# A decoder step on one core: the second norm from per-block sums, rows scaled by a diagonal product, a written order in front of the MLP, and sample values as one run per step

## The chip, the cores and the metric

One core of one Trainium2 chip runs the whole step in one launch. The metric is the device time of one execution in microseconds (us), lower is better. Engines are named as the profile names them: PE (matrix engine; PEld is its weight load), DVE (vector), ACT (scalar), POOL (GpSimd) and SP (the queue that issues most loads).

## The reference, cut to what matters

One layer, 256 prompt tokens and 8 sample tokens (one new token each, with states), D = 2048, FF = 8192, all in float32.

```python
h = rmsnorm(x, g_pre_mix) * (1 + sc1) + sh1
z = h @ w_in                       # three mixers: gMLP gating, HGRN2, GLA
merged = sum(sigmoid(z_gate[n]) * (branch[n] @ w_branch[n]) for n in range(3))
out = merged @ w_out
x = x + gt1 * rmsnorm(out, g_post_mix)
h2 = rmsnorm(x, g_pre_mlp) * (1 + sc2) + sh2
y2 = square(relu(h2 @ w_mlp_up)) @ w_mlp_down
x = x + gt2 * rmsnorm(y2, g_post_mlp)
```

`sh1, sc1, gt1, sh2, sc2, gt2` are six slices of `silu(c) @ w_ada + b_ada`, one row for the prompt and one for each sample. The outputs are the new rows, the final HGRN2 and GLA states of the prompt, the updated states of the samples (`f*S + k v^T`), and the normalised gating rows.

## The kernel before, in words

**Products.** Activations lie with channels on the partitions: 16 channel tiles of 128, each with 264 columns (256 prompt tokens, 8 samples). Every weight block is split into a rounded part `whi` (ACT copy, L112) and a remainder `wlo` (DVE subtract, L109), the activations likewise, and each 128x128 weight tile takes three products (L543 to L545). `granule` (L533) works off one 512 KB block of weights: 24 products. `linear` (L601) makes 256 output columns from 16 channel tiles in four granules, 96 products, and calls `background` after each. `Stream` (L482) keeps blocks loaded up to 5 granules ahead and split up to 2 ahead; there are buffers for 6 half blocks of split weights, and at the end of each granule `ahead` emits the split of the block three further on, into the buffers that this granule gives free.

**Side work.** `background` (L588) advances a granule counter `now` and pumps three queues of generators, in this order: the mixers (`bg`), the samples' states (`bs`) and the remaining rounds of `w_ada` (`ba`), each at a rate in `RATES`. `slot` (L556) puts waiting small products of the mixers and the samples on PE, and one step of an `ada_round` (L275: four products of 128x512 against the condition, eight records in the trace).

**Samples.** `samples_r` (L943) takes one step per sample and 512 state columns. A step fetches the state two steps ahead, asks for the values one step ahead (`values`, L961: a DMA on POOL's queue that hands one sample's value rows, kept in DRAM as `vs_d`, to all 128 partitions), waits until `now` is `FETCHED` = 3 granules past both issues, scales (ACT L983), adds (DVE L985), writes the state back, and queues the products with `q` for a slot. There are four state buffers, so a fetch waits on POOL until the products of an earlier sample (L576) have run. `finish` (L1179) is called in front of a branch: it drains the queues, closes the samples' output with a norm (L995 to L997) and transposes it on PE (L1186). `bs` and `ba` are drained there without granules in between.

**Around the change.** After the third branch comes `w_out`: eight blocks of `linear`, each followed by `gated_rows` (L1293): squares of the block (ACT), the block times the gate (ACT and DVE), four transposes to token rows (L711) and their copies to `og` (L1304, L1312). The last block's squares stay apart and go into the norm's sums as separate products (L1319, L1321: nine of them). `norms` then computes `r1 = rsqrt(mean)` by a bit trick and three Newton rounds on DVE (`rstd_small`, L178: eleven small instructions). The rows are `x1 = x + og*r1` (L1349), the second norm squares `x1` on ACT (L212), sums the samples' squares on DVE and PE, and runs `rstd_small` again; the rows times `r2` (L1358, L1359) are transposed (32 transposes, L228), and `modulate` (L354) makes `h2`, its rounded part and its remainder. Into that stretch `fill` puts steps of the sixth `ada_round`; its first 12 of 32 weight tiles were loaded during `w_out` (`N_PRE`), the others go through two buffers `araw`. What is left of the round goes to `ba` and runs beside the MLP at 0.2 steps per granule. Then `up(0)`, `up(1)`, `down(0)`, and so on.

**Order.** From the start of the mixers to the end of the last branch PE and POOL run in written order (`manual_schedule`), and the compiler's scheduler orders the other engines. From L1283 on it orders all engines by its own estimate. At the end `norms` runs a third time, and eight pieces of 128x512 (L1416, all DVE) make the output rows, which SP and ACT write.

Of the kernel before, what the change touches and what calls it, by code (L numbers as in the profile page):

```python
# [15 lines left out]
P = 128  # L16
# [20 lines left out]
RATES = ((1.7, 0.4, 0.27), (1.5, 0.4, 0.27), (1.2, 0.4, 0.27), (1.0, 0.4, 0.27))  # L37
# [11 lines left out]
FILL = (4.0, 4.0)  # L49
# [11 lines left out]
def hybrid_step_kernel(  # L61
# [141 lines left out]


    def norm_rows(x, xs, xsn, r):
# [148 lines left out]
    def modulate(dst, src, xs, k0, n, A, B, hi, lo):  # L354

        for j in range(n):
            k = k0 + j
            if j % 2 == 0:
                V.tensor_scalar(dst[:, j, 0:NP], src[:, j, :], A[:, k, 0:1], B[:, k, 0:1], ALU.mult, ALU.add)
            else:  # L360
                S.activation(dst[:, j, 0:NP], src[:, j, :], AF.Identity, scale=A[:, k, 0:1], bias=B[:, k, 0:1])
# [87 lines left out]
    def plan():  # L449

        out, k0 = [], 0
        for n in CHUNKS:
            for gi in range(0, len(begin), 4 // n):
                out.append((win, k0, n, begin[gi][0], 4 // n * CW))
            k0 += n
        for c0 in (6144, 6400, 6656, 6912):
            out += blocks(win, 0, KT, c0)
        out += blocks(win, 0, KT, 9216, P)
        for s in range(4):
            out += blocks(win, 0, KT, 7168 + s * CW)  # L460
        for n in range(N_BRANCH):
            if n:
                g0 = 5120 if n == 1 else 8192
                for s in range(4):
                    out += blocks(win, 0, KT, g0 + s * CW)
            for m in range(8):
                out += blocks(win, 0, KT, 9232 + n * D + m * CW) + blocks(w_branch[0, n], 0, 8, m * CW)
        for m in range(8):
            out += blocks(w_out[0], 0, KT, m * CW)
        for f in range(NFB + 1):  # L470
            if f < NFB:
                for m in range(FB // CW):
# [393 lines left out]
    vs_d = dp.tile([3, 8, NS, P], F32, tag="vs_d", name="vs_d")  # L866
# [76 lines left out]
    def samples_r(G):  # L943
# [4 lines left out]
        fs = tmp([P, 4, NS], f"fs{G.i}", 1)  # L948
# [24 lines left out]
        for n, (b, h0) in enumerate(steps):  # L973
# [6 lines left out]
            yield lambda: now[0] >= max(ahead[0][1], vals[0][1]) + FETCHED  # L980
# [20 lines left out]
    def mixer_r(G):  # L1001
# [12 lines left out]
        nc.gpsimd.dma_start(vs_d[G.i, 0:4 * nj].rearrange("k b v -> (k b) v"), vs)  # L1014
# [276 lines left out]
    parts = []  # L1291

    def gated_rows(m, src, Gv, rows):  # L1293
# [4 lines left out]
        g = tmp([P, 2, NP], "gt")  # L1298
        S.activation(g[:, 0, :], src[:, 0, 0:NP], AF.Copy, scale=Gv[:, k, 0:1])
        V.tensor_scalar(g[:, 1, :], src[:, 1, 0:NP], Gv[:, k + 1, 0:1], None, ALU.mult)  # L1300
        pt = to_tokens(g)
        mul(gs[:, k:k + 2, :], src[:, :, NP:NT], Gv[:, k:k + 2, 1:NC])
        c0 = (m % 4) * CW
        S.copy(rows[0][m // 4][:, c0:c0 + CW].rearrange("p (m f) -> p m f", m=2), pt[:, 0])  # L1304
        if m == 0:
            add(sqacc, sq[:, 0, :], sq[:, 1, :])
        elif m < 7:
            add(sqacc, sqacc, sq[:, 0, :])
            add(sqacc, sqacc, sq[:, 1, :])
        else:  # L1310
            parts[:] = [sqacc, sq[:, 0, :], sq[:, 1, :]]
        V.tensor_copy(rows[1][m // 4][:, c0:c0 + CW].rearrange("p (m f) -> p m f", m=2), pt[:, 1])  # L1312

    def norms():

        ps = sm([P, 2 + NS])
        for t in range(2):
            for i, v in enumerate(parts):
                T.matmul(ps[:, t:t + 1], v[:, t * P:(t + 1) * P], ones[:, 0:1], start=i == 0, stop=i == 2)  # L1319
        for i, v in enumerate(parts):  # L1320
            T.matmul(ps[:, 2:2 + NS], ones, v[:, NP:NT], start=i == 0, stop=i == 2)  # L1321
        r = tmp([P, 2 + NS], "nr", 1)
        rstd_small(ps, 1.0 / D, r)
        return r[:, 0:2], r[:, 2:2 + NS]

    og = [[blk([P, 1024]) for _ in range(2)] for _ in range(2)]
    mH, mL = tiles(mh), tiles(ml)
    pre = []
    for m in range(8):
# [6 lines left out]
        gated_rows(m, linear(w_out[0], 0, KT, m * CW, CW, mH, mL), G1, og)  # L1336
# [4 lines left out]
    fill = Queue()  # L1341
    fill.g.append(ada_round(5, pre))
    r1, r1s = norms()
    fill.pump(FILL[0])
    mul(gs, gs, r1s.unsqueeze(1).to_broadcast([P, KT, NS]))
    add(xsT, xsT, gs)
# [9 lines left out]
    for hf in range(2):
        for c in (slice(0, 512), slice(512, 1024)):
            S.activation(xn[0][hf][:, c], x1[0][hf][:, c], AF.Copy, scale=rx[:, 0:1])  # L1358
            V.tensor_scalar(xn[1][hf][:, c], x1[1][hf][:, c], rx[:, 1:2], None, ALU.mult)  # L1359
        for k in range(8 * hf, 8 * hf + 8, 2):  # L1360
            ps = transposed(xn, k)
            q, js = k // 4, slice(k % 4, k % 4 + 2)
            modulate(tmp([P, 2, NT], "vt"), ps, xsn, k, 2, A2, B2, h2h[q][:, js, :], h2l[q][:, js, :])
    ba.g.insert(0, fill.g[0]) if fill.g else None
# [24 lines left out]
    def down(f, ah, al):  # L1389
        for m in range(8):  # L1390
# [20 lines left out]
    r3, r3s = norms()  # L1411
    for t in range(2):
        for hf in range(2):
            for c0 in (0, 512):
                y = yt[t][hf][:, c0:c0 + 512]
                V.scalar_tensor_tensor(y, y, r3[:, t:t + 1], x1[t][hf][:, c0:c0 + 512], ALU.mult, ALU.add)  # L1416
# [58 lines left out]
```

## Time and profile before

| | |
|---|---|
| median of 3 runs | 1991.88 us (1988.23 to 1992.91) |
| profiled execution | 1991.31 us, of which its span is 1989.5 us |
| mean granted PE clock | 0.986 |
| DVE busy | 1190.4 us (60%) |
| ACT busy | 995.5 us (50%) |
| POOL busy, nearly all of it issuing DMAs | 86.0 us (4%) |
| `w_out` stage | about 1090 to 1183 us |
| last branch starts | about 929 us |
| read from HBM, written | 427.60 MB, 11.70 MB |

Times in the profile count from the start of the span. Matrix products are pipelined: a record of L543 lasts 0.28 us, but the next one starts 0.12 us later, so "busy" PE says little and the pace has to be read from start times or from the number of records in a stretch. `xN` is a number of instructions; in brackets or behind a bar stands how long the engine sat idle before a group and what ended most of that idle time. In the windows view `PEclk` is the clock granted to PE as a share of full speed. L-numbers are lines of the kernel before.

### The profile page before, as it was taken

To read this page: it belongs to the slowest core of one execution; us is meant where nothing else is said; L and a number is where in the kernel's file an instruction comes from. 1 tells how busy PE (TensorE), PEld (TensorE's weight loads), DVE (VectorE), ACT (ScalarE), POOL (GpSimd) and SP (SyncE) were. 2 spreads that over 40 slices of the span, in tenths; PEclk is the share of its full clock that TensorE was granted. 3 is DMA by queue.
4 is the path that set the end of the run, shared out by engine and by line. 5 is a ranking of instruction groups with operands and counts; after the bars stand their busy time and mean duration, and the time that the engine had idled before them with its cause. 6 is when DMAs were issued, how large, how long until landed. Compare 5 with 4: busy or idle time off the path is not lost.

```text
span 1989.5 us, 42035 instructions
## 1 busy us (share of the span) xinstructions
PE 1927.4 (97%) x16972; PEld 1819.9 (91%) x16972; DVE 1190.4 (60%) x2092; ACT 995.5 (50%) x1773; POOL 86.0 (4%) x128
## 2 busy tenths in 40 slices
PE   6999999999999999998999999999999999999997
PEld 4889999889989988997999987999999999999996
DVE  3566667685666684455555556544555555555665
ACT  5434354665845754644444545444444445454543
POOL 1000000101101111110000000000000000000000
PEclk8999999999999999999999998999999999999998
DMA  9797797788678788688877755676565555555552
GB/s 311 273 331 250 248 297 220 219 258 251 203 233 255 230 245 258 209 270 260 268 240 228 265 186 157 214 224 200 180 181 181 181 181 182 180 183 181 182 175 96
DMA packets 341267, 442.05 MB, mean 222 GB/s; under 512 B 14930, under 2 KB 285008, under 8 KB 341072
## 3 DMA queue, kind: packets, MB, share of 16 engines
q1 hardware_dynamic: 330880, 409.19, 64.3%
q0 software_dynamic: 9120, 28.91, 5.9%
q8 instruction: 133, 2.18, 0.5%
q10 hardware_dynamic: 1072, 1.25, 0.2%
q14 instruction: 62, 0.51, 0.1%
HBM read 427.60 MB, written 11.70 MB: 221 GB/s over the span
## 4 chain that ended last, share of the span: by engine, by line
PE 92%; DMA 4%; DVE 2%; ACT 1%; issue 1%; SPq 0%; POOL 0%; DVEq 0%; ACTq 0%
PE mm L543 28%; PE mm L544 27%; PE mm L545 27%; PE ada L291 3%; DMA araw<-in_w_ada_dram 1%; PE ada L261 1%; DMA b<-in_w_ada_dram 1%; PE sm L711 1%; PE sm L569 1%; DMA raw<-in_w_in_dram 1%; DVE wlo L109 1%; PE sm L228 0%; DMA st<-in_state_gla_dram 0%; PE sm L576 0%; PE sm L1087 0%
## 5 line engine op out<-in xcount | busy, mean ns | idle before, releaser
L543 PE MATMUL mm<-b,whi 128*128 128x264 f32 x4624 | 1328.3, 287 | 7.3 <-DVE b L106 3.4
L544 PE MATMUL mm<-b,whi 128*128 128x264 f32 x4624 | 1320.1, 285 | 0.2 <-DVE b L109 0.2
L545 PE MATMUL mm<-b,wlo 128*128 128x264 f32 x4624 | 1316.7, 285 | 2.5 <-DVE wlo L109 2.4
L109 DVE TENSOR_TENSOR wlo<-raw,whi 128x512 fp32r<-128x512 f32 x1136 | 777.1, 690 | 596.4 <-ACT whi L112 583.4
L112 ACT CAST whi<-raw 128x512 fp32r<-128x512 f32 x1136 | 695.1, 618 | 762.6 <-PE mm L544 665.6
L543 PEld LDWEIGHTS mm<-b,whi 128*128 128x128 f32 x4624 | 873.8, 189 | 65.4 <-ACT whi L112 27.9
L545 PEld LDWEIGHTS mm<-b,wlo 128*128 128x128 f32 x4624 | 873.6, 189 | 3.9 <-DVE wlo L109 3.8
L544 PEld LDWEIGHTS mm<-b,whi 128*128 128x128 f32 x4624 | 873.3, 189 | 1.6 <-issue 0.8
L106 DVE TENSOR_TENSOR b<-b,mm 128x528 f32<-128x528 f32 x136 | 95.6, 704 | 45.1 <-PE mm L545 45.1
L291 PE MATMUL ada<-araw,cT 128*32 128x512 f32 x464 | 72.9, 621 | 7.5 <-DMA araw<-in_w_ada_dram 7.5
L985 DVE SCALAR_TENSOR_TENSOR st<-vbc,b,st 128x128 f32<-128x128 f32 (+1 forms) x96 | 34.0, 393 | 74.5 <-DMA vbc<-vs_d 69.1
L983 ACT ACTIVATE st<-st,fs 128x128 f32<-128x128 f32 (+1 forms) x96 | 36.9, 430 | 69.0 <-DMA st<-in_state_gla_dram 40.2
L261 PE MATMUL ada<-b,cT 128*32 128x256 f32 (+1 forms) x640 | 36.6, 362 | 9.5 <-DMA b<-in_w_ada_dram 9.0
L261 PEld LDWEIGHTS ada<-b,cT 128*32 128x32 f32 x640 | 18.0, 115 | 23.3 <-DMA b<-in_w_ada_dram 8.4
L103 DVE TENSOR_TENSOR b<-b,b 128x512 f32<-128x512 f32 (+1 forms) x47 | 34.1, 744 | 1.6 <-ACT b L1048 0.7
L291 PEld LDWEIGHTS ada<-araw,cT 128*32 128x32 f32 x464 | 11.9, 109 | 18.9 <-DMA araw<-in_w_ada_dram 11.5
L986 POOL DMA_DIRECT2D out_dram<-st x32 | 23.5, 735 | 111.1 <-DVE st L985 77.5
L109 DVE TENSOR_TENSOR b<-gt,b 128x528 fp32r<-128x528 f32 x32 | 22.7, 708 | 3.2
L963 POOL DMA_DIRECT2D vbc<-vs_d x32 | 24.2, 755 | 5.0 <-DMA vs_d<-sqs 4.6
L112 ACT CAST whi<-araw 128x512 fp32r<-128x512 f32 x20 | 12.4, 621 | 23.0 <-PE mm L544 21.4
L109 DVE TENSOR_TENSOR b<-b 128x1024 f32<-128x1024 f32 (+1 forms) x21 | 22.4, 1068 | 1.4 <-PE sm L569 0.9
L103 DVE TENSOR_TENSOR gt<-vt 128x528 f32<-128x528 f32 x32 | 22.4, 701 | 0.0
(285 smaller groups left out, 808.1 us busy)
## 6 DMA issues: line engine op xcount, KB each, us to landing
raw<-in_w_in_dram SPq DMA_DIRECT2D x232, 512.0 KB, 4.8
raw<-in_w_mlp_up_dram SPq DMA_DIRECT2D x128, 512.0 KB, 3.9
raw<-in_w_mlp_down_dram SPq DMA_DIRECT2D x128, 512.0 KB, 3.6
araw<-in_w_ada_dram SPq DMA_DIRECT2D x116, 512.0 KB, 5.5
b<-in_w_ada_dram SPq DMA_DIRECT2D x60, 512.0 KB, 7.6
raw<-in_w_branch_dram SPq DMA_DIRECT2D x48, 512.0 KB, 4.9
raw<-in_w_out_dram SPq DMA_DIRECT2D x32, 512.0 KB, 4.3
b<-in_w_ada_dram SPq DMA_DIRECT2D x32, 256.0 KB, 6.2
```

The source lines that it names most:

```text
L103: V.tensor_tensor(o, a, b, op=ALU.mult)
L106: V.tensor_tensor(o, a, b, op=ALU.add)
L109: V.tensor_tensor(o, a, b, op=ALU.subtract)
L112: S.copy(hi, src)
L261: T.matmul(acc[32 * j:32 * j + 32, 0:n], cT[:, k, :], w[:, n * j:n * j + n], start=k == 0, stop=k == KT - 1)
L291: T.matmul(acc[32 * j:32 * j + 32, :], cT[:, k, :], ws[j // 2][:, j % 2 * 512:j % 2 * 512 + 512], start=k == 0, stop=k == KT - 1)
L543: T.matmul(o, a, xh(k + j), start=first and j == 0, stop=False)
L544: T.matmul(o, a, xl(k + j), start=False, stop=False)
L545: T.matmul(o, b, xh(k + j), start=False, stop=last and j == n - 1)
L963: nc.gpsimd.dma_start(v, vs_d[G.i, h * nj:h * nj + 4, b, :].partition_broadcast(P))
L983: S.activation(st[:, i, :], st[:, i, :], AF.Copy, scale=fs[:, h0 + i, b:b + 1])
L985: V.scalar_tensor_tensor(st[:, i, :], v[:, i, :], k[:, h0 + i, NP + b:NP + b + 1], st[:, i, :], ALU.mult, ALU.add)
```

## The change

1. *Sums per block.* `gated_rows` is cut in two. `gated` makes the gated block and the squares, `put_rows` the rows. In `w_out`, `put_rows` also gathers per token and block the sums of `x*og` (DVE, with an accumulated output) and of `og*og` (ACT), and runs one granule later (`later`). The first norm's sums of `x*x` are kept (`xx0`). The second norm's sum is then `xx0 + 2*r1*sum(x*og) + r1^2*sum(og*og)`; `x1` isn't needed for it.
2. *Diagonal product.* Instead of scaled rows and a transpose, PE multiplies row tiles by a diagonal matrix: `h2` columns are `x1 @ diag(r2)`, for the first four channel tiles `x @ diag(r2) + og @ diag(r1*r2)`. `x1` is made per 512 columns (`residual`), for the first four channel tiles only after the first MLP blocks.
3. *Written order.* PE in `w_out`, then PE, DVE and ACT until the first two blocks of the MLP are done. The MLP begins with two blocks side by side (`begin_up`, weight blocks of 2 tiles x 512 columns), and each group of four channel tiles is prepared (`quad`) two granules before its use. Six steps of the `ada_round` are placed by hand.
4. *Square root by table.* The norms in front of the MLP and at the end take `Sqrt` on ACT, a reciprocal and one Newton round (`rstd_sqrt`); the table is called for once during block 7 of `w_out`. The last block's squares are added to the others, which leaves three sum products of nine.
5. *Samples.* `vs_d` is ordered so that the values of a step are one contiguous run of 2 KB (before: four of 512 B); the values' wait is one granule shorter, and the queue's rate is 0.5 in place of 0.4. `fs` shares two buffers.
6. *POOL* takes small elementwise work: the samples' columns in front of the MLP, and the adding for two of the eight output pieces, whose scaling goes to ACT.

```diff
-RATES = ((1.7, 0.4, 0.27), (1.5, 0.4, 0.27), (1.2, 0.4, 0.27), (1.0, 0.4, 0.27))
+RATES = ((1.7, 0.5, 0.27), (1.5, 0.5, 0.27), (1.2, 0.5, 0.27), (1.0, 0.5, 0.27))
+    def rstd_sqrt(ms, scale, out):
+        S.activation(out, ms, AF.Sqrt, scale=scale, bias=eps)
+        V.tensor_scalar(xx, ms, scale, EPS, ALU.mult, ALU.add)
+        V.reciprocal(out, out)
+        mul(aa, out, out)
+        V.scalar_tensor_tensor(aa, aa, -0.5, xx, ALU.mult, ALU.mult)
+        V.scalar_tensor_tensor(out, aa, 1.5, out, ALU.add, ALU.mult)
...
-            nc.gpsimd.dma_start(v, vs_d[G.i, h * nj:h * nj + 4, b, :].partition_broadcast(P))
+            r0 = 4 * nj * b + h * nj
+            nc.gpsimd.dma_start(v, vs_d[G.i, r0:r0 + 4, :].partition_broadcast(P))
...
-            yield lambda: now[0] >= max(ahead[0][1], vals[0][1]) + FETCHED
+            yield lambda: now[0] >= max(ahead[0][1] + FETCHED, vals[0][1] + FETCHED - 1)
...
+    def put_rows(m, g, pt, rows, x=None):
+        c0 = (m % 4) * CW
+        if x:
+            for t in range(2):
+                xr = x[t][m // 4][:, c0:c0 + CW].rearrange("p (m f) -> p m f", m=2)
+                V.scalar_tensor_tensor(g[:, 1, 0:CW].rearrange("p (m f) -> p m f", m=2), xr, 1.0, pt[:, t], ALU.mult, ALU.mult, accum_out=sums[:, 0, t, m:m + 1])
+        S.copy(rows[0][m // 4][:, c0:c0 + CW].rearrange("p (m f) -> p m f", m=2), pt[:, 0])
+        if x:
+            for t in range(2):
+                S.activation(g[:, 0, 0:CW].rearrange("p (m f) -> p m f", m=2), pt[:, t], AF.Square, accum_out=sums[:, 1, t, m:m + 1])
+        V.tensor_copy(rows[1][m // 4][:, c0:c0 + CW].rearrange("p (m f) -> p m f", m=2), pt[:, 1])
...
+    next(fill)
+    next(fill)
+    g = gated(7, z, G1)
+    nc.gpsimd.tensor_tensor(sp[:, 0], gs, xsT, op=ALU.mult)
+    nc.gpsimd.tensor_tensor(sp[:, 1], gs, gs, op=ALU.mult)
+    r1 = norms()
+    put_rows(7, g, to_tokens(g), og, x1)
+    next(fill)
+    next(fill)
+    T.matmul(ps.rearrange("p s k b -> p (s k b)"), ones, sp.rearrange("p s k b -> p (s k b)"), start=True, stop=True)
+    V.reduce_sum(both[:, :, 0:2], sums, axis=mybir.AxisListType.X)
+    V.reduce_sum(both[:, :, 2:2 + NS], ps.rearrange("p s k b -> p s b k"), axis=mybir.AxisListType.X)
+    for _ in range(FILL):
+        next(fill)
+    mul(q, both[:, 1], r1)
+    V.scalar_tensor_tensor(q, both[:, 0], 2.0, q, ALU.mult, ALU.add)
+    mul(q, q, r1)
+    add(q, q, xx0)
+    V.tensor_scalar(q, q, 0.0, None, ALU.max)
+    rstd_sqrt(q, 1.0 / D, r2)
+    for t in range(2):
+        V.tensor_scalar(dg[:, t, :], ident, r2[:, t:t + 1], None, ALU.mult)
+    for t in range(2):
+        V.tensor_scalar(dg[:, 2 + t, :], dg[:, t, :], r1[:, t:t + 1], None, ALU.mult)
...
+    def residual(q):
+        cs = slice(q % 2 * 512, q % 2 * 512 + 512)
+        for t in range(2):
+            x = x1[t][q // 2][:, cs]
+            V.scalar_tensor_tensor(x, og[t][q // 2][:, cs], r1[:, t:t + 1], x, ALU.mult, ALU.add)
+    def quad(q):
+        if q:
+            residual(q)
+        for i2 in range(2):
+            ps = sm([P, 2, NP])
+            for i in range(2):
+                c0 = q % 2 * 512 + (2 * i2 + i) * P
+                for t in range(2):
+                    o = ps[:, i, t * P:(t + 1) * P]
+                    T.matmul(o, x1[t][q // 2][:, c0:c0 + P], dg[:, t, :], start=True, stop=q > 0)
+                    if q == 0:
+                        T.matmul(o, og[t][0][:, c0:c0 + P], dg[:, 2 + t, :], start=False, stop=True)
+            js = slice(2 * i2, 2 * i2 + 2)
+            modulate(tmp([P, 2, NT], "vt"), ps, xsn, 4 * q + 2 * i2, 2, A2, B2, h2h[q][:, js, :], h2l[q][:, js, :], nc.gpsimd)
+    quad(0)
+    ba.g.insert(0, fill)
...
+    def begin_up():
+        accs = [new_acc(), new_acc()]
+        for k in range(0, KT, 2):
+            if k % 4 == 0 and k + 4 < KT:
+                quad(k // 4 + 1)
+            granule(w_mlp_up[0], 0, 2, 0, 2 * CW, accs, h2H, h2L, k, k == 0, k + 2 == KT)
+            if k >= 8:
+                background()
...
+                if hf == 1 and c0 == 0:
+                    S.activation(y, y, AF.Copy, scale=r3[:, t:t + 1])
+                    nc.gpsimd.tensor_tensor(y, y, x1[t][hf][:, c0:c0 + 512], op=ALU.add)
+                else:
+                    V.scalar_tensor_tensor(y, y, r3[:, t:t + 1], x1[t][hf][:, c0:c0 + 512], ALU.mult, ALU.add)
```

In `modulate` every fourth channel tile is scaled on DVE and the three others on ACT, where before the two engines took turns.

More of the change, by code (lines that the diff above doesn't have):

```diff
@@ L48 @@
 N_BRANCH = 3
-FILL = (4.0, 4.0)
+FILL = 3
 READY = object()
@@ L471, in plan @@
             if f < NFB:
-                for m in range(FB // CW):
+                if f == 0:
+                    out += blocks(w_mlp_up[0], 0, KT, 0, 2 * CW)
+                for m in range(0 if f else 2, FB // CW):
                     out += blocks(w_mlp_up[0], 0, KT, f * FB + m * CW)
@@ L586, in slot @@
                 add(os_, os_, po)
+    later = []
     def background():
         now[0] += 1
+        while later and later[0][0] < now[0]:
+            later.pop(0)[1]()
         bg.pump(rate[0])
@@ L1013, in mixer_r @@
         yield 0.2
-        nc.gpsimd.dma_start(vs_d[G.i, 0:4 * nj].rearrange("k b v -> (k b) v"), vs)
+        nc.gpsimd.dma_start(vs_d[G.i, 0:4 * nj * NS, :], vs)
         def vr(t, h):
@@ L1290, in hybrid_step_kernel, with gated @@
     gs = tmp([P, KT, NS], "gs", 1)
-    parts = []
-    def gated_rows(m, src, Gv, rows):
+    def gated(m, src, Gv):
         k = 2 * m
@@ L1317, in norms @@
         for t in range(2):
[L1318 to L1321, printed above, removed]
+            T.matmul(ps[:, t:t + 1], sqacc[:, t * P:(t + 1) * P], ones[:, 0:1], start=True, stop=True)
+        T.matmul(ps[:, 2:2 + NS], ones, sqacc[:, NP:NT], start=True, stop=True)
         r = tmp([P, 2 + NS], "nr", 1)
-        rstd_small(ps, 1.0 / D, r)
-        return r[:, 0:2], r[:, 2:2 + NS]
+        rstd_sqrt(ps, 1.0 / D, r)
+        return r
+    order = tc.manual_schedule(engines={mybir.EngineType.PE})
+    order.__enter__()
     og = [[blk([P, 1024]) for _ in range(2)] for _ in range(2)]
     mH, mL = tiles(mh), tiles(ml)
+    sums = tmp([P, 2, 2, NS], "fs")
     pre = []
+    fill = ada_round(5, pre)
     for m in range(8):
@@ L1335, in hybrid_step_kernel @@
                 pre.append(w)
-        gated_rows(m, linear(w_out[0], 0, KT, m * CW, CW, mH, mL), G1, og)
+        z = linear(w_out[0], 0, KT, m * CW, CW, mH, mL)
+        if m < 7:
+            g = gated(m, z, G1)
+            later.append((now[0], lambda m=m, g=g: put_rows(m, g, to_tokens(g), og, x1)))
+        if m == 6:
+            S.activation(tmp([P, 1], "srr", 1), sqacc[:, 0:1], AF.Sqrt)
     ba.drain()
@@ L1340, in hybrid_step_kernel @@
     B2 = mod[:, 3 * KT:4 * KT, :]
[L1341 to L1346, printed above, removed]
+    order.__exit__(None, None, None)
+    order = tc.manual_schedule(engines={mybir.EngineType.PE, mybir.EngineType.DVE, mybir.EngineType.Activation})
+    order.__enter__()
+    next(fill)
+    next(fill)
+    g = gated(7, z, G1)
+    sp = tmp([P, 2, KT, NS], "os2", 1)
+    nc.gpsimd.tensor_tensor(sp[:, 0], gs, xsT, op=ALU.mult)
@@ L1347, in hybrid_step_kernel @@
+    for _ in range(FILL):
+        next(fill)
+    q = tmp([P, 2 + NS], "rr", 1)
+    mul(q, both[:, 1], r1)
[3 more added lines that the diff above has]
+    V.tensor_scalar(q, q, 0.0, None, ALU.max)
+    r2 = tmp([P, 2 + NS], "rr0", 1)
+    rstd_sqrt(q, 1.0 / D, r2)
+    dg = tmp([P, 4, P], "gt")
     for t in range(2):
-        for hf in range(2):
-            V.scalar_tensor_tensor(x1[t][hf], og[t][hf], r1[:, t:t + 1], x1[t][hf], ALU.mult, ALU.add)
@@ L1350, in hybrid_step_kernel @@
-    rx = tmp([P, 2], "rx", 1)
+        V.tensor_scalar(dg[:, t, :], ident, r2[:, t:t + 1], None, ALU.mult)
+    for t in range(2):
+        V.tensor_scalar(dg[:, 2 + t, :], dg[:, t, :], r1[:, t:t + 1], None, ALU.mult)
     xsn = tmp([P, KT, NS], "xsn", 1)
-    norm_rows(x1, xsT, xsn, rx)
-    fill.pump(FILL[1])
-    xn = [[blk([P, 1024]) for _ in range(2)] for _ in range(2)]
+    nc.gpsimd.tensor_tensor(gs, gs, r1[:, 2:2 + NS].unsqueeze(1).to_broadcast([P, KT, NS]), op=ALU.mult)
+    nc.gpsimd.tensor_tensor(xsT, xsT, gs, op=ALU.add)
@@ L1355, in hybrid_step_kernel @@
+    nc.gpsimd.tensor_tensor(xsn, xsT, r2[:, 2:2 + NS].unsqueeze(1).to_broadcast([P, KT, NS]), op=ALU.mult)
     h2h, h2l = [blk(dt=F32R) for _ in range(4)], [blk(dt=F32R) for _ in range(4)]
[L1356 to L1363, printed above, removed]
@@ L1397, in down @@
             if f == NFB - 1:
-                gated_rows(m, dst, G2, yt)
-    pend = up(0)
+                g = gated(m, dst, G2)
+                put_rows(m, g, to_tokens(g), yt)
+    zs = begin_up()
+    order.__exit__(None, None, None)
+    residual(0)
+    pend = up(0, zs)
     for f in range(NFB):
```

49 lines of the change are left out of this document (28 added, 21 removed).

## The prediction

> **What bounds the kernel now.** I read the busy shares first, then the chain of work that ended last, then the groups by line.
>
> ```profile
> PE 1927.4 (97%) x16972; PEld 1819.9 (91%) x16972; DVE 1190.4 (60%) x2092; ACT 995.5 (50%) x1773; POOL 86.0 (4%) x128
> ...
> PE 92%; DMA 4%; DVE 2%; ACT 1%; issue 1%; SPq 0%; POOL 0%; DVEq 0%; ACTq 0%
> ```
>
> PE is on the chain for 92% of the span, and the change takes no weight product away. So it can win only where PE waits, runs at a lower clock, or does other work. I looked for such places in PE's timeline in front of the MLP, in PE's waits, and behind the last product.
>
> ```profile
> 1183.03 0.29 PE L545 MATMUL mm<-b,wlo 128*128 128x264 f32 x1
> 1183.24 1.90 PE L291 MATMUL ada<-b,cT 128*32 128x512 f32 x10
> ...
> 1187.57 4.06 PE L291 MATMUL ada<-b,cT 128*32 128x512 f32 x35
> ...
> 1196.64 1.36 PE L291 MATMUL ada<-araw,cT 128*32 128x512 f32 x2 [3.71 <-DMA araw<-in_w_ada_dram]
> ```
> ```profile
> 1236.89 0.61 ACT L1375 ACTIVATE vt<-mm 128x528 f32<-128x528 f32 x1
> ...
> 1260.19 0.61 ACT L1375 ACTIVATE vt<-mm 128x528 f32<-128x528 f32 x1
> 1273.04 0.61 ACT L1375 ACTIVATE vt<-mm 128x528 f32<-128x528 f32 x1
> ```
> ```profile
> 1240.00:1400.00 160.00, 7.45 (x54) 1.00 0.68 212
> ```
>
> *The gap.* `w_out` ends at 1183.3. L1375 starts when a block of the MLP is done: every 11.65 us, and 12.85 us where one step of the sixth `ada_round` (8 records of L291) runs beside it, so a step costs 1.2 us there. One pitch ahead of 1236.89 the first block ended, at 1225.2: the gap is 1225.2 - 1183.3 - 11.65 = **30.3 us** without MLP products. The last fence is the windows view of L291 alone: 54 of the round's 128 records, 6.75 steps or 8.1 us, are left for the MLP. Gap and rest together: 38.4 us.
>
> ```profile
> PE sm L1186 <- ACT os L997: 5.0, 1, 5.0
> PE mm L545 <- DVE wlo L109: 2.4, 2, 1.5
> ```
> ```profile
> 928.00:930.00 2.00, 1.18 (x6) 0.50 0.03 11
> ...
> 934.00:936.00 2.00, 2.00 (x17) 0.90 0.77 256
> ```
>
> *The samples in front of branch 3.* PE waits 5.0 us for the samples' closing norm, and the windows (length, PE busy with its count, granted clock, DMA share, GB/s) show a clock of 0.50 from about 928 to 934: 5.5 us at half pace are 2.7 us more. This place costs **7.7 us**.
>
> **Part by part.**
>
> *Samples (part 5): -7.* By the code the third sample group, two steps per sample, goes round like this: the products flush, the next granule takes the first step, the second waits three granules for its values, and the products wait four more unless an `ada` step calls a slot earlier: 8 granules.
>
> ```profile
> 860.59 0.71 POOL L958 DMA_DIRECT2D st<-in_state_gla_dram  x1 [14.36 <-PE sm L576]
> ...
> 887.12 0.71 POOL L958 DMA_DIRECT2D st<-in_state_gla_dram  x1 [15.40 <-PE sm L576]
> ```
>
> The fetches that wait for a flush are 26.5 us apart, 3.3 us per granule. One granule less per round is 8 x 3.3 = 26 us over the eight samples. Two flushes come after 887: by themselves they would fall at 914 and 940, but the branch forces the last just ahead of its wait. A granule less per round moves the last to about 914, and the closing norm is over before the branch asks. The higher rate helps a little at the start only; a held queue keeps no more than one unit. I take 7.0 of the 7.7, since the branch's own DVE and ACT burst at 929 to 937 loses the cover of the slow clock. Bounds: 0 and -7.7.
>
> *Values as one run: 0.*
>
> ```profile
> vbc<-vs_d POOLq DMA_DIRECT2D x32, 256.0 KB, 8.1
> ...
> st<-in_state_hgrn_dram POOLq DMA_DIRECT2D x16, 256.0 KB, 5.8
> st<-in_state_gla_dram POOLq DMA_DIRECT2D x16, 256.0 KB, 5.4
> ```
> ```profile
> DVE st L985 <- DMA vbc<-vs_d: 69.1, 20, 5.9
> ```
>
> Values land 8.1 us after issue. State rows, with runs of 512 B (HGRN2) and 1 KB (GLA), land after 5.8 and 5.4: run length is worth 0.4 there, so I expect 7 to 8 us. DVE sits idle 69.1 us for values, but splits run two granules ahead and PE waits for `wlo` only 2.4 us in all, so most of it is covered. The wait one granule shorter eats cover, the landing gives some back: 0, bounds -4 and +4.
> By the Trainium skill, "DMA: Bandwidth & Descriptors", Specifications, transfers reach line rate from 512 B on, so the old runs were long enough and the new layout would save nothing; the 5.8 beside 5.4 agrees, and 8.1 shows that something else slows the values.
>
> *The gap (parts 1 to 4): +0.6.* I set the written queues against each other, from 0 at the end of `w_out`.
>
> ```profile
> 1183.88 0.69 DVE L109 TENSOR_TENSOR wlo<-raw,whi 128x512 fp32r<-128x512 f32 x1 [0.77 <-ACT whi L112]
> ...
> 1189.11 0.17 DVE L189 SCALAR_TENSOR_TENSOR sa<-sa,sx 128x10 f32<-128x10 f32 x1
> 1189.32 0.17 DVE L190 SCALAR_TENSOR_TENSOR nr<-sa,nr 128x10 f32<-128x10 f32 x1
> ```
> ```profile
> L106 DVE TENSOR_TENSOR a<-a,vt 128x264 f32<-128x264 f32 x24 | 10.3, 427 | 0.5 <-ACT vt L1297 0.3
> L361 ACT ACTIVATE vt<-sm,mod,A 128x256 f32<-128x256 f32 x8 | 4.5, 562 | 2.9 <-DVE vt L359 1.5 <-DVE vt L103 1.4
> L112 ACT CAST b<-vt 128x528 fp32r<-128x528 f32 x8 | 4.9, 629 | 0.3 <-DVE vt L106 0.2
> L109 DVE TENSOR_TENSOR b<-vt,b 128x528 fp32r<-128x528 f32 x8 | 5.6, 705 | 0.9 <-ACT b L112 0.9
> L1416 DVE SCALAR_TENSOR_TENSOR b<-b,nr,b 128x512 f32<-128x512 f32 x8 | 5.6, 749 | 0.0
> ```
> ```profile
> 356.58 0.89 PE sm L816 x8
> ```
>
> DVE first has the last `wlo` (to 1.3), the block's scaling (1.75), then two adds of 0.43: squares summed at 2.6. Three sum products (0.12 per record, six records, by the row of L1319 further down) and four transposes: 3.9. `r1` needs `Sqrt` and four small instructions at 0.2 each: 4.4. DVE's two accumulating products, a copy and the reduction end at 6.1; meanwhile PE does two fill steps at 1 us each (35 records in 4.06), the samples' sum (6.35), three more steps (9.3). DVE: reduction 6.8, five small instructions 7.8, `Sqrt` and four more 8.9, diagonals from 9.2. So this part keeps PE filled but for 1.6 us; all of the sixth round's steps here come from tiles already loaded, and the 3.71 us wait for `araw` goes.
> A 128x128 product takes 0.22 (4 in 0.89), so the 16 of `quad(0)` end at 13.1. Then what is late next: DVE's remainder for the second pair ends at 13.1 + 0.56 + 0.46 + 0.63 + 0.70 = 15.5, and only behind it in DVE's queue come the two 512-column pieces of `residual(1)`, to 16.2 and 16.9. `quad(1)` stands on PE in front of the first MLP granule, so PE idles 3.1 us, and the products begin at **18.3**.
> `quad(2)` and `quad(3)` meet the same queue: they follow a granule whose end emits the next split. Its second half finds buffers only when that granule ends; 0.62 + 0.69 later DVE reaches `residual`, and PE gets its second piece 2.7 us after the granule. Each costs 2.5 us of waiting and 8 x 0.22 = 1.8: 4.35. The gap is 18.3 + 8.7 = **27.0 us**, 3.3 less. But only six `ada` steps run in it; ten remain at 1.2 = 12.0 in place of 8.1. Together 39.0, +0.6. Bounds: without the three `residual` waits -7.9, with the clock rival below +4.
>
> *Small and hidden.* In `w_out` each block adds two DVE products (about 0.5 each) and two ACT squares (0.37 plus 0.19 for the read of the sum).
>
> ```profile
> 1085.00:1183.30 98.30, 98.28 (x804) 96.70 (x807) 57.33 (x103) 49.23 (x87) 0.00 (x0) 1.00 0.72 236
> ```
>
> DVE is busy 57.3 of 98.3 us there, ACT 49.2; 8 more each fit under PE's blocks. Uncovered, a block would pay about 1 us. One load of the `Sqrt` table, 1.28 us by any `ACT_TABLE_LOAD`, lies there too. POOL's elementwise work isn't in the trace of before: nearest below is `memset`,
>
> ```profile
> 0.88 0.95 POOL L865 MEMSET att<- 128x1024 f32 x1
> ```
>
> 0.95 us for 1024 columns, which is 0.1 to 0.2 for 128; above, I allow 1 us per instruction, with which the samples' columns (three instructions after `r2` at 8.9) are ready at 11.9, when the rounding of the first pair begins. Near enough to `memset` they cost 0; at 2 us each, +3.
>
> *The end (parts 4 and 6): -3.5.*
>
> ```profile
> 1974.58 1.42 PE sm L1319 x12
> 1976.00 1.30 PE sm L1321 x6
> ...
> 1979.78 1.41 DVE b L1416 x2
> ```
>
> Nine sum products in 2.7 us become three (0.9) with two adds first that run beside the transposes: -1.8. Eleven small instructions become one on ACT and four: -1.2. Two of eight output pieces leave DVE, -1.3, but POOL's second piece and its DMA behind three others on ACT may end last and take 0.8 back. -3.5, bounds -5 and -1.
>
> **Sum:** 0.6 - 7 + 0 - 3.5 = -9.9 on the profiled 1991.31: 1981.4. The median of the runs is 0.57 above that execution, so **1982**.
>
> **Rivals.**
> *The gap closes as written* (0.2): `residual` isn't late, if DVE does the remainders sooner than I set them. For it: three of four channel tiles go to ACT. Against: every wait above is a queue order. 8.1 us less, **1974**.
> *The samples still come late* (0.13): 26 us is just what is needed, and the slot's timing may round it away. Then 7 are missing: **1989**.
> *The clock falls in front of `quad(1)`* (0.1):
>
> ```profile
> 1198.00:1200.00 2.00, 2.00 (x9) 0.63 (x8) 1.20 (x8) 0.00 (x0) 0.00 (x0) 0.50 0.04 8
> ```
>
> the idle 3.71 us before 1196.64 was followed by this half clock (0.50 in the row). With 3.1 us idle the products could start at half pace for some 6 us: +3, **1985**.
> The Trainium skill, "TensorE: Matmul & The Clock Gate", Part 1, puts the bound at one idle window of about 3.4 us; by that 3.1 just escapes.
> *Values block DVE, slower* (0.07): DVE takes `vbc` in order, and the `wlo` behind it feed PE. The longest such wait was 5.9 us (the last number of its row),
>
> about the two granules (5.8) by which splits lead. A granule less makes it 9.2, so 3.4 us of PE idle and up to 2.7 at half clock. Four such steps of 32 decide it: 25 us, **2006**.
>
> **How the numbers follow.** The forecast has 0.45, with 1976 to 1988 for its own bounds; 0.05 is left for a shift in the scheduler's order elsewhere. A difference below 0.3% (6 us) can't be told from none here. Faster by more needs 1985.9 or less: 0.8 of the forecast, the closed gap, half of the clock rival, little else: 0.65. Slower by more: the last rival and a little: 0.08. The range takes in closed gap and late samples, 1972 to 1990.
>
> **What would show it.** In the trace of after: no wait of L1186's transposes for the samples' norm, and no half clock at 929; PE's wait in front of `quad(1)` about 3 us and two of about 2.5 for `residual`; first MLP product some 18 us after `w_out`; ten `ada` steps after it; values landing in 7 to 8 us; a stretch from the last weight product to the end that is 3.5 us shorter. Wrong would be: PE waiting for POOL in the gap, or `wlo` waits of several us between 380 and 900.

## The result and the profile after

The changed kernel takes 1980.76 us (median of 4 runs, 1977.6 to 1982.0), the kernel before 1991.83 us beside it: a ratio of 0.9945, 95% interval 0.9928 to 0.9962, so 8 to 14 us faster. The forecast was 1982. The profiled execution has a span of 1979.2 us (before: 1989.5). The sum came out; its terms did not, and their errors hid each other.

Busy shares and the chain of work that ended last, after:

```profile
PE 1922.9 (97%) x16996; PEld 1824.0 (92%) x16996; DVE 1192.0 (60%) x2087; ACT 1000.6 (51%) x1804; POOL 91.3 (5%) x152
...
PE 93%; DVE 2%; ACT 2%; DMA 2%; issue 1%; POOL 0%; SPq 0%; DVEq 0%; ACTq 0%; POOLq 0%
```

DMA's part of the chain has halved (4% before). The table follows one and the same record through both traces: how much earlier (-) or later it starts after the change, and what the stage itself adds.

| stage (time in the trace of before) | offset at its end, us | stage alone, us |
|---|---|---|
| to 331, the head | -3.3 | -3.3 |
| 331 to 924, branches 1 and 2 | -1.3 | +2.0 |
| 924 to 945, start of branch 3 | -9.5 | -8.2 |
| 945 to the end of `w_out` | -10.6 | -1.2 |
| gap and the rest of the sixth `ada` round, to 1467 | -10.0 | +0.6 |
| the rest of the MLP | -8.1 | +1.9 |
| last weight product to the end | -10.3 | -2.2 |

The head moves by 3 us in kernels that change nothing there (the shorter wait alone, below: -3.2; the run alone: +0.4); I don't count it to the change. Without it the stages add up to -7.0, while whole executions gain 11: one pair of traces shows where time went, and the runs below weigh the parts. The 1.2 and 1.9 come back in all eight traces with the new gap (0.6 to 1.7 gained in `w_out`, 0.9 to 2.0 lost in the rest of the MLP) and hardly in those without it (at most 0.3 and 0.6 lost), so they belong to the change outside the samples; why is not explained.

The start of branch 3, windows view of after (length; busy time and count of PE, PEld, DVE, ACT, POOL; granted clock; DMA share; GB/s):

```profile
926.00:928.00 2.00, 2.00 (x21) 1.86 (x22) 2.00 (x5) 2.00 (x3) 1.13 (x2) 1.00 0.38 107
928.00:930.00 2.00, 2.00 (x17) 1.16 (x17) 2.00 (x4) 0.66 (x2) 0.53 (x1) 1.00 0.81 252
```

Before, this place had 5.0 us of wait for the samples' norm and then a clock of 0.50. Both are gone: PE is busy in both windows, at 1.00.

The waits of PE from 300 to 950 us, after (us in total, times, longest):

```profile
PE sm L590 <- DVE b L103: 5.4, 2, 3.8
PE mm L566 <- DVE wlo L109: 3.6, 1, 3.6
PE sm L1200 <- ACT b L1202: 2.1, 1, 2.1
```

The waits for `araw` are gone from this list, but one of 3.6 us for a low half (`wlo`, 2.4 in two before) and one of 2.1 us for blocks from ACT are in it. Hold on to these two.

The gap, PE's timeline of after (start, length, instruction, idle before it with its releaser):

```profile
1172.60 1.07 PE L309 MATMUL ada<-b,cT 128*32 128x512 f32 x8
1176.04 0.61 PE L1352 MATMUL sm<-cst,a 128*128 128x1 f32 x4 [2.37 <-DVE a L106]
...
1188.77 2.19 PE L309 MATMUL ada<-araw,cT 128*32 128x512 f32 x8
1192.20 2.40 PE L1443 MATMUL sm<-gt,b 128*128 128x128 f32 x16 [1.24 <-DVE b L1431]
1194.36 0.37 PE L564 MATMUL mm<-b,whi 128*128 128x264 f32 x1
...
1200.35 1.07 PE L309 MATMUL ada<-araw,cT 128*32 128x512 f32 x8
1202.45 0.46 PE L1443 MATMUL sm<-gt,b 128*128 128x128 f32 x2 [1.03 <-PE ada L309]
...
1210.62 1.06 PE L309 MATMUL ada<-araw,cT 128*32 128x512 f32 x8
1212.76 2.40 PE L1443 MATMUL sm<-gt,b 128*128 128x128 f32 x16 [1.07 <-DVE b L1431]
```

In front of `quad(1)`, `quad(2)` and `quad(3)` stands an `ada` step (x8 of L309) and 1.1 to 1.2 us of idle time (1.03 and another 0.16 in front of `quad(2)`). The first MLP product comes 21.8 us behind `w_out`. Records of L309 that are left for the MLP, windows view of that line alone:

```profile
1240.00:1400.00 160.00, 6.39 (x48) 0.94 (x48) 1.00 0.66 205
```

48 records, six steps, not the ten that the prediction left over. The code takes no step between the written six and `quad(3)`, so the compiler's scheduler must have put four more there.

The values, DMA issues of after (count, KB each, median us to landing), and below them DVE's waits for them:

```profile
vbc<-vs_d POOLq DMA_DIRECT2D x32, 256.0 KB, 6.4
```
```profile
DVE st L1012 <- DMA vbc<-vs_d: 50.6, 18, 5.3
```

8.1 and 69.1 before. The end, DVE's timeline of after:

```profile
1968.74 1.41 DVE L1523 SCALAR_TENSOR_TENSOR b<-b,nr,b 128x512 f32<-128x512 f32 x2
1970.07 1.35 DVE L103 TENSOR_TENSOR gs<-gs,nr 128x128 f32<-128x128 f32 x1
1971.34 1.75 DVE L1523 SCALAR_TENSOR_TENSOR b<-b,nr,b 128x512 f32<-128x512 f32 x1
1973.01 0.36 DVE L106 TENSOR_TENSOR sqs<-gs,xsT 128x128 f32<-128x128 f32 x1
1973.22 2.06 DVE L1523 SCALAR_TENSOR_TENSOR b<-b,nr,b 128x512 f32<-128x512 f32 x3
```

Six pieces and the samples' two products take 6.5 us. The same eight pieces and products before:

```profile
1979.78 1.41 DVE L1416 SCALAR_TENSOR_TENSOR b<-b,nr,b 128x512 f32<-128x512 f32 x2
1981.11 0.29 DVE L103 TENSOR_TENSOR gs<-gs,nr 128x128 f32<-128x128 f32 x1
1981.31 0.75 DVE L1416 SCALAR_TENSOR_TENSOR b<-b,nr,b 128x512 f32<-128x512 f32 x1
...
1982.18 3.39 DVE L1416 SCALAR_TENSOR_TENSOR b<-b,nr,b 128x512 f32<-128x512 f32 x5
```

Eight pieces took 5.8. After, the second and third instruction run long, 1.35 for 0.29 and 1.75 for 0.75, and both start while POOL adds (1969.60 to 1972.54).

### The profile page after: what moved, and what is told of

Read it like the earlier page. It is cut to its first block, busy times and chain, and to the rows that moved or that the text cites. A ratio compares the mean times of both kernels' runs of the same rounds, so it can differ in the third digit from the quotient of the medians.

```text
span 1979.2 us, 42117 instructions
## 1 busy us (share of the span) xinstructions
PE 1922.9 (97%) x16996; PEld 1824.0 (92%) x16996; DVE 1192.0 (60%) x2087; ACT 1000.6 (51%) x1804; POOL 91.3 (5%) x152
## 4 chain that ended last, share of the span: by engine, by line
PE 93%; DVE 2%; ACT 2%; DMA 2%; issue 1%; POOL 0%; SPq 0%; DVEq 0%; ACTq 0%; POOLq 0%
PE mm L564 29%; PE mm L565 28%; PE mm L566 28%; PE ada L309 3%; PE ada L279 1%; PE sm L736 1%; PE sm L590 1%; ACT whi L112 1%; PE sm L597 1%; DMA raw<-in_w_in_dram 1%; PE sm L1114 1%; DMA b<-in_x_prompt_dram 0%; DVE wlo L109 0%; PE sm L1443 0%; DMA vbc<-vs_d 0%
## 5 line engine op out<-in xcount | busy, mean ns | idle before, releaser
L309 PE MATMUL ada<-araw,cT 128*32 128x512 f32 x464 | 64.3, 603 | 0.1
L1479 ACT ACTIVATE b<-vt 128x528 fp32r<-128x528 f32 x32 | 20.7, 646 | 1.0
```

Of the source, the lines that this page charges most:

```text
L309: T.matmul(acc[32 * j:32 * j + 32, :], cT[:, k, :], ws[j // 2][:, j % 2 * 512:j % 2 * 512 + 512], start=k == 0, stop=k == KT - 1)
```

## The experiments

The runs form four groups, each timed beside the kernel before. Its median was 1995.0, 1992.6, 1997.2 and 1992.2 us in them, so ratios are compared, not times.

### First group: the samples' three edits

**Samples alone.** The kernel before with all of part 5 but the shared `fs`: the run, the shorter wait, the rate of 0.5.

> The kernel before with the three samples' edits alone (values as one run, values' wait 2 granules, rate 0.5). If the gain is PE's wait for the samples' norm in front of branch 3 and the half clock behind it: that wait is gone and the time is about 1984 us (some 8 below before), with the gap in front of the MLP as before (30 us). If the gain comes from the gap and the norms instead: 1990 to 1992.

1983.8 us, 0.9949 [0.9934, 0.9964]; the 5.0 us wait is gone. Nearly the whole gain of the change.

**Everything but the samples.** The changed kernel with these three edits taken back.

> The changed kernel with the three samples' edits undone. By the samples theory the 5 us wait and the half clock at the start of branch 3 come back: about 1988 to 1989 us, and what is left below before (2 to 4 us) is the end of the kernel and the written order in w_out. By the gap theory: about 1981, the gain stays.

1994.4 us, 0.9991 [0.9973, 1.0010]. The wait is back, word for word the old one, here in the list of PE's waits:

```profile
PE sm L1211 <- ACT os L1022: 5.0, 1, 5.0
```

Gap and end by themselves are worth nothing that can be measured. In its trace, 7 us behind at 945 already, `w_out` gains 1.6 us and the end 2.5, and gap and MLP together lose 2.8.

**The wait alone**, on the kernel before:

```diff
-            yield lambda: now[0] >= max(ahead[0][1], vals[0][1]) + FETCHED
+            yield lambda: now[0] >= max(ahead[0][1] + FETCHED, vals[0][1] + FETCHED - 1)
```

> The kernel before with the values' wait one granule shorter, nothing else. By the prediction's stepping 8 rounds of one granule less move the last flush from 940 to 914 us, just enough: wait in front of branch 3 gone, about 1984 us. Rival: the shorter wait alone is rounded away by the slots' timing and the rate of 0.4 holds the queue: last flush after 915, some of the 5 us wait stays, 1988 to 1992.

1978.1 us, 0.9925 [0.9903, 0.9947]. No wait in front of branch 3; the last product of the third sample group starts at 890 us (923 before), and from 924 to 945 us the trace gains 8.2. Whole executions gain more, 15 us (11 to 19). The profiled one was the slowest of the four and ends 9.9 ahead, 3.2 of it from the head, so what the others gain beyond this stage isn't placed.

**The rate alone**, on the kernel before: 0.5 for 0.4 in the four entries of `RATES`.

> The kernel before with the samples' rate 0.5 in place of 0.4, nothing else. By the prediction the rate helps little, since the steps wait for granules and slots: last flush still forced at about 923, the 5 us wait stays, 1990 to 1992 us. Rival: the rate is what holds the rounds at 8 granules; then the last flush falls to about 890 and the time to 1984.

1994.2 us, 1.0005 [0.9991, 1.0019]; the 5.0 us wait stays. By this run the rate is worth nothing. That holds for the kernel before, and, as the last runs show, only for it.

### Second group: the run, the residual, the output pieces

**The run alone**, on the kernel before (the write to `vs_d` and the copy into `srow` follow the new order too):

```diff
-            nc.gpsimd.dma_start(v, vs_d[G.i, h * nj:h * nj + 4, b, :].partition_broadcast(P))
+            r0 = 4 * nj * b + h * nj
+            nc.gpsimd.dma_start(v, vs_d[G.i, r0:r0 + 4, :].partition_broadcast(P))
```

> The kernel before with only the values' layout changed (one run of 2 KB per step). By the prediction 0 in time, since the values' wait is covered: 1990 to 1995 us with the 5 us wait in front of branch 3 still there; values land in 7 to 8 us by the prediction, in 6.2 to 6.4 if the layout alone makes the landing seen in the changed kernel.

1979.4 us, 0.9941 [0.9922, 0.9960]: it went against the prediction. The longest waits of PE from 640 to 945 us, first before, then the run alone:

```profile
PE sm L1186 <- ACT os L997: 5.0, 1, 5.0
PE ada L291 <- DMA araw<-in_w_ada_dram: 3.8, 3, 1.6
PE mm L545 <- DVE wlo L109: 2.4, 2, 1.5
```
```profile
PE sm L1188 <- ACT os L999: 5.0, 1, 5.0
PE ada L291 <- DMA araw<-in_w_ada_dram: 0.8, 1, 0.8
```

The wait for the norm stays. What goes are waits for *other* transfers and for the splits behind them: by its weight products the trace is 1.6 us ahead at 688, 9.4 at 899 and 12.0 at 945. The DMA queue that carries the values, same window (packets, MB, share of the 16 engines' time), before and with the run:

```profile
q0 software_dynamic: 4845, 16.02, 20.2%
```
```profile
q0 software_dynamic: 4769, 15.77, 15.6%
```

Nearly the same bytes take 4.6% of 305 us less on the mean of the 16 engines, 14 us; the values land 6.5 us after issue (8.1). ACT's waits for blocks of `w_in`, which the splits need, in the same window, before and with the run:

```profile
ACT whi L112 <- DMA raw<-in_w_in_dram: 18.0, 9, 4.2
```
```profile
ACT whi L112 <- DMA raw<-in_w_in_dram: 3.4, 3, 1.8
```

The other traces divide in the same way. In the four kernels with four short runs this wait is 11.6 to 20.4 us, PE's wait for `araw` 3.2 to 4.0, the median landing of `araw` 6.6 to 6.9 and the queue's share 20.0 to 20.2%; in the ten with one long run they are 0 to 9.6, 0 to 0.8, 5.3 to 6.4 and 15.6 to 16.2%. So the layout decides both, the time that the values take on the DMA engines and how late the other operands are. That the first causes the second is my reading; no run changes that time alone. DVE also stands less long at the values (28.1 us for 38.9 in this window), and the `wlo` part may come from there.

PE's waits are only part of the gain. PE stands still 6.1 us in this window for 13.4 before, and the half clock that gave 0.91 over 740 to 760 us before doesn't appear with the run (1.00), which is worth 1.8.

**Output pieces on DVE.** The changed kernel without POOL's adds.

```diff
-                if hf == 1 and c0 == 0:
-                    S.activation(y, y, AF.Copy, scale=r3[:, t:t + 1])
-                    nc.gpsimd.tensor_tensor(y, y, x1[t][hf][:, c0:c0 + 512], op=ALU.add)
-                else:
-                    V.scalar_tensor_tensor(y, y, r3[:, t:t + 1], x1[t][hf][:, c0:c0 + 512], ALU.mult, ALU.add)
+                V.scalar_tensor_tensor(y, y, r3[:, t:t + 1], x1[t][hf][:, c0:c0 + 512], ALU.mult, ALU.add)
```

> The changed kernel with all eight output pieces on DVE again. If POOL's adding slows DVE beside it (one piece took 1.75 us and the samples' product 1.35 there, against 0.75 and 0.29 before), DVE's stretch from the norm to its last piece falls from 6.5 to 5.8 us and the end comes some 0.7 us sooner. If POOL really takes work off DVE, the end comes 1.3 us later.

1981.2 us, 0.9944: no difference in the median, none was in reach. The trace tells it, DVE's timeline of this kernel:

```profile
1970.70 1.42 DVE L1519 SCALAR_TENSOR_TENSOR b<-b,nr,b 128x512 f32<-128x512 f32 x2
1972.04 0.28 DVE L103 TENSOR_TENSOR gs<-gs,nr 128x128 f32<-128x128 f32 x1
1972.24 0.74 DVE L1519 SCALAR_TENSOR_TENSOR b<-b,nr,b 128x512 f32<-128x512 f32 x1
```

The long two are short again; from the first piece to the end of the span it is 9.6 us, 10.4 with POOL in the same group. Eight pieces on DVE are 0.8 us quicker than six on DVE and two on POOL, and all traces agree: 9.6 in three, 10.4 in five.

**Residual early.** The changed kernel with `residual(1)` ahead of the products of `quad(0)`, and `residual(2)` and `(3)` at the end of the quad before.

```diff
-        if q:
-            residual(q)
+        if q == 0:
+            residual(1)
...
+        if 0 < q < 3:
+            residual(q + 1)
```

> The changed kernel with each residual written one group sooner (the first in DVE's idle 2.6 us in front of quad 0, the next two at the end of the group before). If PE's waits for residual lengthen the gap, the three waits of 1.0 to 1.2 us go, the first MLP product comes 3 to 4 us sooner after w_out (18 instead of 21.8), some ada steps that filled those waits move into the MLP at 1.2 us each, and the time falls by about 4 us against the changed kernel of the same call. If the ada steps in the waits already hide them: within 1 us.

1975.6 us, 0.9922 [0.9904, 0.9940]. Beside it ran the changed kernel as it is:

> The changed kernel as it is, beside the others on the same chip: 0.9945 of before, as measured; its gap 54.7 us from the end of w_out to the end of the second MLP block.

1980.6 us, 0.9946 [0.9928, 0.9964]. The intervals overlap; the trace with the residuals early is clear, PE's waits in the gap:

```profile
PE sm L1352 <- DVE a L106: 2.4, 1, 2.4
PE sm L1443 <- DVE b L1431: 0.2, 1, 0.2
```

2.5 us in three waits have become 0.2 in one, and two waits of 1.5 in all, which the trace puts down to the `ada` steps in front of `quad(0)` and `quad(2)`, are gone too. Three of the `ada` steps that had filled the holes go into the MLP. From the end of `w_out` to 1467 us the trace gains 3.1 us on the kernel before, where the changed kernel in the same group loses 0.6: 3.7 us. So the place of `residual` in DVE's queue was the price, as the prediction said.

### Third and fourth group: do the gains add, and what does the rate do

**Run and wait, rate left at 0.4**, on the kernel before.

> The kernel before with the layout (values as one run per step) and the wait for the values one unit shorter, the planner's rate for pool steps left at 0.4. The run alone gave 1979.4 and kept the 5.0 us wait in front of branch 3; the wait edit alone gave 1978.1 and lost it. Theory A, two separate stores (the run takes 8 us of stalls on araw and wlo out of 690 to 900 us, the wait edit takes 7.7 us out in front of branch 3): the gains add, 1972, TensorE idle between 300 and 945 us falls from 13 us in the run alone to 7 or 8. Theory B, one store (steps that are released sooner only move the stalls): at 1979 as each alone, with idle of 13 us or more. A result near 1972 also says that the rate of 0.5 costs some 8 us in the changed kernel.

1966.7 us, 0.9854 [0.9833, 0.9874]. The gains add, and a little more. From 640 to 945 us PE is busy all but 0.2 of 305 us. With the rate of 0.5 the same two edits gave 0.9949 in the first group: by that the rate costs 0.95%, some 19 us.

**Residual early and pieces on DVE**, both on the changed kernel:

> The changed kernel with two of its own edits amended: the residual of quad 1 before quad 0's products and those of quads 2 and 3 at the end of the quad before (alone 1975.6), and all eight output pieces on VectorE (alone, the tail 0.9 us shorter). Separate places, so they should add: 1980.7 less 3.7 to 5.0 less 0.9, 1975 to 1976; the residual waits gone (0.2 us in all), norm to end 9.6 us. Rival: the output pieces bring nothing measurable, 1976 to 1977.

1975.7 us, 0.9897 [0.9875, 0.9919].

**The same with the rate at 0.4:**

> The kernel of the run beside it (residuals early, output pieces on VectorE) with the planner's rate for pool steps back at 0.4. If the rate of 0.5 costs 8 us where the run and the wait have taken the stalls (theory A of the layout and wait run), 1967 to 1969. If the rate is worth nothing either way, as the rate alone was on the kernel before (1.0005), 1975 like the run beside it. If the rate is needed together with the shorter wait, the 5.0 us wait in front of branch 3 comes back, 1982.

1961.5 us, 0.9829 [0.9805, 0.9852], against 1975.7 in the same group: the rate of 0.5 costs 14 us here. This kernel beats both, 1.7% faster than before.

**The changed kernel, rate alone put back:**

```diff
-RATES = ((1.7, 0.5, 0.27), (1.5, 0.5, 0.27), (1.2, 0.5, 0.27), (1.0, 0.5, 0.27))
+RATES = ((1.7, 0.4, 0.27), (1.5, 0.4, 0.27), (1.2, 0.4, 0.27), (1.0, 0.4, 0.27))
```

> The changed kernel with one number put back, the planner's rate for pool steps (0.4 for 0.5); gap, tail, run and wait stay as changed. By the pair of runs that differ in the rate alone (ratios 0.9897 and 0.9829 of the kernel before) the rate of 0.5 costs 13 us in the changed kernel: 1967 here, the waits of TensorE for the low halves in front of 701 us and for the blocks in front of 826 us gone. If the 13 us belong only to the amended gap and tail, 1980 as the changed kernel. The gap and the tail as written are then read as the difference from the kernel before with run and wait alone (0.9854): by the run that left the samples' edits out, nothing to 2 us less; by the prediction's terms (gap +0.6, end -3.5) 2.9 us less.

1965.4 us, 0.9870 [0.9850, 0.9890], where the changed kernel has 0.9945: the rate costs 15 us. Gap and end as written add nothing to run and wait (0.9870 beside 0.9854, in different groups). PE's waits from 300 to 950 us, with the rate at 0.4:

```profile
PE sm L590 <- DVE b L103: 3.7, 1, 3.7
PE sm L826 <- DVE srow L822: 1.7, 1, 1.7
```

The waits for `wlo` and for ACT's blocks are gone, so they came with the rate. Where they start is seen on DVE, with the rate at 0.5 (the changed kernel), then at 0.4:

```profile
682.52 0.69 DVE L109 TENSOR_TENSOR wlo<-raw,whi 128x512 fp32r<-128x512 f32 x1 [1.21 <-ACT whi L112]
687.29 0.69 DVE L109 TENSOR_TENSOR wlo<-raw,whi 128x512 fp32r<-128x512 f32 x1 [4.07 <-ACT whi L112]
689.03 0.88 DVE L1012 SCALAR_TENSOR_TENSOR st<-vbc,b,st 128x256 f32<-128x256 f32 x2 [1.05 <-DMA vbc<-vs_d]
...
690.53 1.31 DVE L1281 SCALAR_TENSOR_TENSOR b<-b,vec,b 128x1056 f32<-128x1056 f32 x1
...
697.24 2.50 DVE L1054 TENSOR_TENSOR_SCAN b<-cst,b 128x264 f32<-128x264 f32 x4
```
```profile
681.45 0.70 DVE L1270 SCALAR_TENSOR_TENSOR b<-b,mm 128x528 f32<-128x528 f32 x1
682.18 1.32 DVE L1281 SCALAR_TENSOR_TENSOR b<-b,vec,b 128x1056 f32<-128x1056 f32 x1
...
688.21 2.50 DVE L1054 TENSOR_TENSOR_SCAN b<-cst,b 128x264 f32<-128x264 f32 x4
```

At 0.5 the first step of the third sample group stands on ACT and DVE *ahead* of the branch's own burst (L1281 to the scan L1054), before its transfers have landed. ACT waits for it,

```profile
685.84 0.91 ACT L1010 ACTIVATE st<-st,fs 128x256 f32<-128x256 f32 x2 [3.34 <-DMA st<-in_state_gla_dram]
```

with the next `whi` behind it; DVE idles 4.07 and 1.05 us (the 1.21 ahead of them is a table load on ACT), and when the burst then runs, the low halves are late: 3.6 us of wait on PE, and a clock of 0.91 over 680 to 720 us. At 0.4 the burst is over before the step's product, which DVE first has at 708 us, and DVE doesn't idle there. ACT still waits 5.26 us for state rows, but at 717 us, behind the burst, where PE shows no wait for it. All six traces with run, wait and the rate of 0.5 have a wait of 3.6 us for `wlo` and a clock below 1.00 in 680 to 720 or 800 to 840 us; the three with 0.4 have neither. In numbers, from the windows view over 300 to 945 us, at 0.5 and then at 0.4:

```profile
300.00:945.00 645.00, 631.50 (x6194) 585.89 (x6193) 421.70 (x802) 369.95 (x728) 73.06 (x111) 0.99 0.76 241
```
```profile
300.00:945.00 645.00, 639.01 (x6330) 594.12 (x6329) 431.66 (x820) 377.50 (x740) 73.06 (x111) 1.00 0.78 249
```

PE idles 13.5 us at 0.5 and 6.0 at 0.4 (20.0 before); the windows 680 to 720 and 800 to 840, at 0.91 and 0.96 for 1.00, hold another 5.2. That is 12.7 of the 16.7 us by which the two traces stand apart at 945; the rest isn't placed.

## Why the prediction was right, step by step

By the runs the parts of the change are worth: the shorter wait -15 us, the run -12, the rate of 0.5 +15, everything else -2 (between -5 and +2). That is -14, beside -11 for the whole, within the intervals. The forecast had -7, 0, 0 and -2.9. So the total was met by luck: the gains that it did not see (12, and 8 more of the wait) and the loss (15) nearly cancel.

- **The wait in front of branch 3: right in place, too small.** -7 was forecast, at most -7.7; -8.2 is in that stage, and the shorter wait alone does it. Its 15 us by whole executions are more than the place holds, and that part stays open. The last products of the samples came 51 us earlier (872 for 923), not 26: the wait alone gives 33, run and wait at the rate of 0.4 give 49 (874), so the rate adds little.
- **"Values as one run: 0": wrong.** Alone it gives 12 us by the trace, far outside the bounds of 4. The step looked only at who waits *for the values*. It did not ask who waits for the same DMA engines: PE's waits for `araw` and `wlo` in the window fell from 6.2 to 0.8 us, ACT's for `w_in` from 18.0 to 3.4. The landing (7 to 8 us forecast, 6.5 measured alone) was too cautious as well. The comparison with the state rows, 5.8 against 5.4, was between transfers that aren't broadcasts, which may be why; no run shows it. By the Trainium skill, "DMA: Bandwidth & Descriptors", Specifications, runs of 512 B already reach line rate; here four such runs and one of 2 KB differ by 1.6 us in landing, so the measurement decides against that use of the rule.
- **"The higher rate helps a little at the start only": wrong.** It costs 15 us (0.9945 for 0.9870), though only where both run and wait have made the steps ready sooner; on the kernel before it does nothing. So run and rate, 12 gained and 15 lost, left the sum near where the forecast had it.
- **The gap: sum right, parts off.** +0.6 forecast, +0.6 measured, in a trace whose clock stayed at 1.00 there. Where the gap is the same and the clock falls once it is +1.7 and +1.8, where it falls twice +3.4. The first product came 21.8 us behind `w_out` for 18.3, and six `ada` steps were left, not ten. The prediction took a written order to be the whole order; the compiler's scheduler moved four more steps into it. Each `residual` wait was sized at 2.5 to 3.1 us and shows as a step of 1.1 to 2.2 and a wait of 1.1 to 1.2: the same hole, filled in part. The run with the residuals early is the test, 3.7 us of the three holes (8.1 forecast if all of it closed). PE doesn't wait for POOL in the gap, as forecast.
- **The end: -2.2 for -3.5.** From the last product to the first output piece it is 7.8 before and 4.8 after, the -3.0 forecast for sums and norm. That this fits so well is chance: in the six traces with the old sums it is 7.0 to 9.0, in the eight with the new ones 4.6 to 5.0. It is longest where the clock falls at once (0.53 and 0.50 from 1962 to 1966 us with the run alone, 9.0) and short where it stays (1.00 from 1965 to 1967 with the shorter wait alone, 7.1). The term that failed is the two pieces: -0.5 forecast, +0.7 measured, because POOL's adds slow DVE beside them.
- **The rivals.** *Values block DVE* happened once instead of four times: DVE and ACT behind a sample step whose transfers hadn't landed, 3.6 us of idle PE and the lower clock. It is the sign of being wrong that the prediction named, a `wlo` wait of several us between 380 and 900. Its cause was put wrong, though: with the shorter wait and the rate of 0.4 it doesn't appear. *The clock falls in front of `quad(1)`* did not happen in the profiled execution of the changed kernel; it did in that of the kernel with the rate put back (below). *The gap closes* and *the samples still come late* did not happen.

## What to carry to other kernels

Price a transfer by the engine time it takes from the others as well as by who waits for it: a gain can lie with an operand that the edit doesn't touch. Test a tuning number again after the edits it is tuned with; the rate that cost nothing alone cost 15 us once its steps were ready sooner, and a combined change that wins may hide a part that loses. Where an order is written by hand, look for what else may still be put into it.

## What the runs showed of the hardware

**DMA.** 256 KB broadcast to 128 partitions by POOL's queue took 8.1 us to land from four runs of 512 B and 6.5 from one of 2 KB (medians of 32; over all traces 7.6 to 8.1 and 5.9 to 6.5), and the queue's share of engine time over the whole span went from 5.9% to 4.6%, at the same packets and bytes.

**POOL beside DVE.** An add of 128x512 f32 takes POOL 1.49 us, and the two DVE instructions that started beside it ran 1.06 and 1.00 us longer than before. The Trainium skill, "GPSIMD Engine Reference", 1. Specifications, says that POOL contends with DVE instructions that have two SBUF inputs; the trace agrees and gives it a price.

**The clock after short waits.** In the changed kernel with the rate at 0.4, PE stood still for 2.37 us in front of the sum products of the gap, and then (windows of 2 us, clock behind POOL's column):

```profile
1158.00:1160.00 2.00, 1.17 (x10) 1.10 (x10) 0.74 (x2) 0.24 (x1) 1.03 (x2) 0.96 0.74 239
1160.00:1162.00 2.00, 2.00 (x14) 0.44 (x16) 1.57 (x9) 0.17 (x2) 0.81 (x2) 0.50 0.01 3
1162.00:1164.00 2.00, 2.00 (x14) 0.45 (x6) 0.52 (x2) 1.08 (x5) 0.07 (x1) 0.69 0.00 0
```

it ran at 0.50 for a while; the three values below 1.00 are worth (0.04 + 0.50 + 0.31) x 2 = 1.7 us. A second fall behind the wait for `residual(1)`, 1.07 us at 1176, cost as much. The changed kernel has the same 2.37 us wait, at 1176.04, and the clock stayed at 1.00. All eight traces with the new gap have this wait, and behind it the clock fell in six. So the length of one wait doesn't decide it. By the Trainium skill, "TensorE: Matmul & The Clock Gate", Part 1, the clock follows an activity window of 3.4 us that runs free of the program, and one idle window halves it; here it fell behind waits of 2.37 and 1.07 us, so the trace asks for less than a whole idle window.
